# Column halves and quarter tiles in the two recurrent mixers of a four-layer backbone

## The chip, the core and the metric

One core of a Trainium2 chip runs the whole program in one launch. The engines are TensorE (PE in the rows, its weight loads PEld), VectorE (DVE), ScalarE (ACT), GpSimd (POOL) and SyncE (SP, which starts most DMAs). The metric is the device time of one execution in microseconds (us), and the time before is the median of three executions.

## The reference

The program computes four layers on 256 context tokens and 256 latent tokens of width 1024. Each layer is a modulated RMSNorm, a token mixer and a gated residual, then a second norm and a feed-forward part. The mixers are, in order: a bidirectional Mamba-2 scan, a bidirectional RWKV-7 scan, centred pooling, and grouped attention. The change touches the first two. Cut to the lines that matter:

```
# mixer 1, one direction: 32 heads of 64 channels, chunks of 128 tokens
seg   = cum[:, :, :, None] - cum[:, :, None, :]
decay = exp(where(lower, seg, -inf))
cb    = einsum('bcign,bcjgn->bcijg', cm, bm)
w     = cb[..., None] * decay * dt
y     = einsum('bcijge,bcjgep->bcigep', w, x) + (part from the chunks before)
out   = rmsnorm(y * silu(z)) @ out_w            # z = u @ in_w[:, :2048]

# mixer 2, one direction: 16 heads of 64, for every token t
sa = S @ kk_t
S  = S * w_t - outer(sa, kk_t * a_t) + outer(v_t, k_t)
y_t = S @ r_t
```

Mixer 2 is computed in chunks of 64 tokens: products of decayed operands inside a chunk ("grams"), the inverse of a triangular matrix, and a short scan over four chunks.

## The kernel before

The matrix products with weights are made in two parts: `whi` is a weight rounded to fp32r, `wlo` is what is left of it, and each product is three matmuls (L212 to L214). `wsplit` (L200) makes the parts: ScalarE the upper one, and one of the engines in `eng` the lower one (L207).

**Mixer 1** (`mix` and its helpers, L472 to L595). Four groups of eight heads, two steps each. A step takes 256 columns of x (`x_products`), convolves them, and then works on two pairs of heads (`m`). For each head `e` of a pair and each direction `d` it spreads the decays over 128 partitions (L542, L543), takes the exponential on ScalarE (`E`, L548), multiplies it by `cb` on VectorE (`W`, L550), and adds four float32 products into the pair's bank `py` (L553). A head's product has 64 output rows, so it uses one half of TensorE's columns. `gate_z` projects the gate z of a step, with the lower parts of its weights made by the engine in `ZE` (L470), which is GpSimd.

**Mixer 2.** `stage` prepares one direction of a unit (`Unit`: eight heads, of the context, `j` 0, or of the latents, `j` 1). For each chunk, `decays` makes decay products, `operands` the joint operand tile `BK` (two tensors side by side, each head parity with zeros in the rows of the other, L1060 and L1061), `grams` multiplies it (L1077 or L1080) and turns it round (L1089). There are four units with four chunks and two directions each: 32 such steps. `invert` makes the triangular inverse; with `warm` (L1384) it adds 32 products of no use, by `spin` (L1116). `scan` is the recurrence over chunks. Generators of these functions are run in turn by `weave`.

The order on each engine isn't written out by hand: a scheduler places the instructions of all these functions on five queues, each in order, and fills TensorE's queue in mixer 1 with projections of the next step. The pools' buffer counts bound how far it can look ahead.

Of the kernel before, what the change touches and what calls it, by code (L numbers as in the profile page):

```python
# [10 lines left out]
F32 = mybir.dt.float32  # L11
# [4 lines left out]
ALU = mybir.AluOpType  # L16
# [121 lines left out]
def tile_backbone(ctx: ExitStack, tc: tile.TileContext, T, out: bass.AP, dbg=None, stop=99):  # L138
# [227 lines left out]
    with ExitStack() as es:  # L366
# [103 lines left out]
        XE, ZE = (V,), (G,)  # L470
# [25 lines left out]
        def mix(g, s, px, bf, cf, btm, cb):  # L496
# [38 lines left out]
            for m in range(2):  # L535
                mi = 4 * g + 2 * s + m
                py = bank("py", 1)
                for e in range(2):
                    h = hf + 2 * m + e
                    for d in range(2):  # L540
                        pbc = bank("pbc", 2)
                        PE.matmul(pbc, ehb[:, h:h + 1].to_broadcast([96, 128]), parts[d], start=True, stop=False)  # L542
                        PE.matmul(pbc, identb, maskb[:, d:d + 1, :].to_broadcast([128, 4, 128]),  # L543
                                  start=False, stop=True)
                        E = mt.tile([128, NT], F32, name="E")
                        for c in range(4):
                            sl = slice(128 * c, 128 * c + 128)
                            S.activation(E[:, sl], pbc[:, sl], AF.Exp, bias=ncum[:, c, 32 * d + h:32 * d + h + 1])  # L548
                        W = mt.tile([128, NT], F32, name="W")
                        V.tensor_mul(W, E, cb)  # L550
                        for c in range(4):
                            sl = slice(128 * c, 128 * c + 128)
                            PE.matmul(py[64 * e:64 * e + 64, sl], xdt[d][:, c, 128 * m + 64 * e:128 * m + 64 * e + 64],  # L553
                                      W[:, sl], start=d == 0 and c == 0, stop=d == 1 and c == 3,
                                      skip_group_check=True)
                V.tensor_add(yz[:, mi, :], yz[:, mi, :], py)
                for d in range(2):
# [11 lines left out]
                    W = mt.tile([128, NT], F32, name="W")  # L569
# [422 lines left out]
    def stage(tp, rp, F, un, d, l2, nb, bks, tags, ready):  # L992
# [5 lines left out]
        last = 64 if d == 0 else 0  # L998
# [37 lines left out]
        def decays(c):  # L1036
# [7 lines left out]
            S.activation(Dp[:, :, o:o + 64], cum, AF.Exp, scale=-0.3032655)  # L1044
            S.activation(cum, cum, AF.Exp, scale=0.3032655)
            return Dp, cum

        def operands(c, dd, slot):
# [4 lines left out]
            V.tensor_copy(un.dc[d][:, :, c:c + 1], Dp[:, :, last:last + 1])  # L1053
            KR = rp.tile([128, 4, NQ], F32, name=f"KR{slot}")

            BK = bks[d][un.flip[d]]
            un.flip[d] ^= 1
            for par in range(2):
                r, b0 = ROWS[par], 64 * par
                V.scalar_tensor_tensor(BK[par][r, :, b0:b0 + 64], ta[r, :, cl], 0.5, Di[r], op0=ALU.mult, op1=ALU.mult)  # L1060
                G.tensor_mul(BK[par][r, :, 64 - b0:128 - b0], kd[r, :, cl], Di[r])  # L1061
# [4 lines left out]
            return BK  # L1066

        def grams(c, BK, slot):
# [5 lines left out]
            for h in range(4):  # L1074
                for par in range(2):
                    if j:
                        PE.matmul(g[par][:, h, :], BK[par][:, h, :], KR[:, h, :], start=True, stop=True)  # L1077
                    else:
                        for z in range(2):
                            PE.matmul(g[par][ROWS[z], h, :], BK[par][:, h, 64 * z:64 * z + 64], KR[:, h, :],  # L1080
                                      start=True, stop=True)
# [5 lines left out]
            for h in range(4):  # L1087
                for par in range(2):
                    PE.transpose(t[par][:, 64 * h:64 * h + 64], BK[par][ROWS[par], h, :],  # L1089
                                 ident[ROWS[par], ROWS[par]])  # L1090
# [23 lines left out]
    def spin(o, x):  # L1114

        PE.matmul(o[:, :x.shape[1] * x.shape[2]], ident, x, start=True, stop=True)  # L1116

    def invert(tp, un, zbank, slots={}, warm=(0, 0)):

# [69 lines left out]
        for d in range(2):  # L1189
            zb = zbank() if d else z0  # L1190
            z = zb[:, :256].rearrange("p (n t) -> p n t", t=16)
            for n in range(16):
                if warm[0] and n % warm[0] == 0:
                    spin(zb[:, 256:], zp[:, d, n, 0:16].unsqueeze(2).to_broadcast([128, 16, 8]))
                for q in range(4):
                    a, b = (TB[1], zp[:, 1, :, 0:16]) if d else (zp[:, 0], T32[0][:, :, 16:32])
                    PE.matmul(z[QS(q), n, :], a[QS(q), n, :], b[QS(q), n, :], start=True, stop=True)
# [5 lines left out]
        for d in range(2):  # L1203
            cb_ = slice(32 * (1 - d), 32 * (1 - d) + 32)
            z = zbank()
            for n in range(16):
                if warm[1] and n % warm[1] == 0 and n < 13:
                    spin(z[:, 32 * n:], TB[d][:, n, :].unsqueeze(2).to_broadcast([128, 32, 4]))
# [8 lines left out]
        for d in range(2):  # L1217
            cb_ = slice(32 * (1 - d), 32 * (1 - d) + 32)
            z = zbank()
            for n in range(16):  # L1220
                if warm[1] and n % warm[1] == 0 and n < 13:
                    spin(z[:, 32 * n:], T32[d][:, n, :].unsqueeze(2).to_broadcast([128, 32, 4]))
# [85 lines left out]
    def operand_tiles(tp):  # L1308
        t = [[tp.tile([128, 2, 4, 128], F32, name=f"BK{d}{i}") for i in range(2)] for d in range(2)]
        for d in t:  # L1310
            for x in d:
                for par in range(2):
                    G.memset(x[:, par], 0.0)
        return [[[x[:, par] for par in range(2)] for x in d] for d in t]
# [17 lines left out]
    with ExitStack() as es:  # L1332
# [28 lines left out]
        with tc.tile_pool(name="r00", bufs=1, side="right", reuse_waits="tile") as r00, tc.tile_pool(name="tp0", bufs=1, reuse_waits="tile") as tp:  # L1361
# [22 lines left out]
            weave((invert(tp, D0, misc, warm=(2, 4)), 1), *stages(tp, r01, F, D1, 1, bks, (("gr", "xu"), ("acc", "xu")), always))  # L1384
            mark("T01S00")
            slots = {"T": ("BK00", [128, 2, 4, 128]), "M0": ("l2", [128, 2, 512]), "M1": ("BK01", [128, 2, 4, 128])}
# [490 lines left out]
```

## Time and profile before

| | |
|---|---|
| time, median of 3 | 2691.66 us (2684.7 to 2692.46) |
| profiled execution, time | 2704.16 us |
| its span | 2702.3 us, 43164 instructions |
| TensorE, VectorE, ScalarE, GpSimd busy | 92%, 77%, 54%, 15% |
| mean granted TensorE clock | 0.934 |

The stages in the order of time are: mixer 1 (to 478 us), its output projection and the dense feed-forward part (to some 930 us), mixer 2 (to some 1660 us), and then, for nearly all of the remaining 1042 us, the experts, whose weights stream from memory. Within mixer 2 the rows speak of the context's first unit (1005 to 1080), its inverse beside the second unit (1080 to 1165), its scan (1165 to 1240), the latents' first unit (1340 to 1395), and their scan beside the second unit (1440 to 1540). Busy time is that of an engine with at least one instruction in flight. One float32 product of the program stands in the trace as two matmul records (512 for L553, of which the program has 256); a float32 transpose is one.

### The profile page before, as it was taken

The numbers are of one execution on the slowest core, as the hardware profiler recorded it, in microseconds if no ns is written. First come the engines' busy times: TensorE is split into PE (matmuls) and PEld (weight loads), VectorE is DVE, ScalarE is ACT, GpSimd is POOL, SyncE is SP. The second block draws the span as 40 slices with busy tenths as digits, with TensorE's granted clock in tenths as the row PEclk, the third lists the DMA queues.
The fourth block names the chain that finished last, engine by engine and source line by source line (L and its number), as shares of the span: only waits on it lengthen the run. The fifth ranks groups of instructions, "written<-read, shape, count | busy, mean of one in ns | idle before, by whom it ended". The sixth has DMA issues, their size and how long they took to land. (4 is left out here: it accounts for less than half of the span.)

```text
span 2702.3 us, 43164 instructions
## 1 busy us (share of the span) xinstructions
PE 2499.3 (92%) x16810; PEld 2043.9 (76%) x16810; DVE 2070.4 (77%) x3118; ACT 1455.4 (54%) x2290; POOL 416.1 (15%) x506
## 2 busy tenths in 40 slices
PE   7999999999999968768977898999999999999997
PEld 4777776778888867558866687788788788878875
DVE  5777788667454377778696745999899899989997
ACT  4444446333222265336343334878787778778775
POOL 1122132110000156224453221000000000000001
PEclk9999999999999978577887877999999999999998
DMA  7322231335554231012110116699899899989983
GB/s 260 114 86 88 78 102 53 132 110 196 177 196 160 65 110 48 1 42 95 41 63 10 57 34 249 262 360 362 326 372 357 330 362 368 358 320 363 372 340 152
DMA packets 99207, 511.54 MB, mean 189 GB/s; under 512 B 11648, under 2 KB 19072, under 8 KB 55216
## 3 DMA queue, kind: packets, MB, share of 16 engines
q1 hardware_dynamic: 97520, 506.52, 51.1%
q8 instruction: 134, 2.20, 0.3%
q10 hardware_dynamic: 1472, 2.16, 0.3%
q14 instruction: 81, 0.66, 0.1%
HBM read 506.54 MB, written 2.10 MB: 188 GB/s over the span
## 5 line engine op out<-in xcount | busy, mean ns | idle before, releaser
L1734 DVE TENSOR_TENSOR wlo<-wraw,whi 128x1024 fp32r<-128x1024 f32 x662 | 798.4, 1224 | 71.3 <-ACT whi L1733 50.6
L1733 ACT CAST whi<-wraw 128x1024 fp32r<-128x1024 f32 x662 | 694.3, 1051 | 209.2 <-PE gu L214 112.0
L213 PE MATMUL gu<-wlo,xg 128*128 128x512 f32 x896 | 355.7, 397 | 1.5 <-DVE wlo L1734 0.7
L214 PE MATMUL gu<-whi,xg 128*128 128x512 f32 x896 | 350.3, 391 | 0.0
L212 PE MATMUL gu<-whi,xg 128*128 128x512 f32 x896 | 336.8, 392 | 1.1 <-ACT xg L1753 0.9
L206 ACT CAST whi<-wraw 128x1024 fp32r<-128x1024 f32 (+2 forms) x126 | 129.5, 1028 | 229.8 <-PE acc L213 216.4
L207 DVE TENSOR_TENSOR wlo<-wraw,whi 128x1024 fp32r<-128x1024 f32 (+2 forms) x110 | 131.7, 1198 | 106.3 <-ACT whi L206 106.2
L213 PEld LDWEIGHTS gu<-wlo,xg 128*128 128x128 f32 x896 | 168.8, 188 | 42.4 <-DVE wlo L1734 5.8
L212 PEld LDWEIGHTS gu<-whi,xg 128*128 128x128 f32 x896 | 168.7, 188 | 38.2 <-ACT xg L1753 1.6
L214 PEld LDWEIGHTS gu<-whi,xg 128*128 128x128 f32 x896 | 168.9, 188 | 31.6
L213 PE MATMUL y<-wlo,HT 128*128 128x512 f32 x448 | 179.1, 400 | 2.3 <-DVE wlo L1734 2.1
L212 PE MATMUL y<-whi,HT 128*128 128x512 f32 x448 | 177.1, 397 | 3.0 <-DVE xg L1754 3.0
L214 PE MATMUL y<-whi,HT 128*128 128x512 f32 x448 | 176.8, 395 | 0.0
L1808 POOL TENSOR_TENSOR wraw<-yx,SH 128x512 f32<-128x512 f32 x4 | 7.5, 1879 | 1025.4 <-DVE yx L1804 1025.4
L212 PE MATMUL acc<-h2hi,whi 128*128 128x512 f32 x352 | 137.3, 393 | 3.4 <-ACT h2hi L343 3.4
L213 PE MATMUL acc<-h2lo,whi 128*128 128x512 f32 x352 | 137.7, 391 | 0.0
L212 PE MATMUL acc<-hhi,whi 128*128 128x512 f32 (+1 forms) x328 | 135.8, 414 | 0.8 <-ACT whi L206 0.8
L214 PE MATMUL acc<-h2hi,wlo 128*128 128x512 f32 x352 | 135.0, 391 | 0.9 <-DVE wlo L207 0.9
L213 PE MATMUL acc<-hlo,whi 128*128 128x512 f32 (+1 forms) x328 | 134.1, 409 | 0.0
L214 PE MATMUL acc<-hhi,wlo 128*128 128x512 f32 (+1 forms) x328 | 133.8, 409 | 0.0
L305 POOL TENSOR_TENSOR sqa<-sqa,sq 128x512 f32<-128x512 f32 (+1 forms) x35 | 46.8, 1338 | 536.0 <-issue 311.9
L777 POOL TENSOR_TENSOR wlo<-wraw,whi 128x512 fp32r<-128x512 f32 (+1 forms) x69 | 86.1, 1257 | 150.3 <-ACT whi L776 138.9
(575 smaller groups left out, 5550.6 us busy)
## 6 DMA issues: line engine op xcount, KB each, us to landing
wraw<-in_w_mi_dram SPq DMA_DIRECT2D x219, 1024.0 KB, 4.9
wraw<-in_w_mo_dram SPq DMA_DIRECT2D x112, 1024.0 KB, 4.9
wraw<-in_w_modT_dram SPq DMA_DIRECT2D x56, 512.0 KB, 4.1
wraw<-in_w_ffi_dram SPq DMA_DIRECT2D x44, 512.0 KB, 3.6
wraw<-in_w_mod_dram SPq DMA_DIRECT2D x40, 512.0 KB, 4.5
wraw<-in_w_mb_dram SPq DMA_DIRECT2D x40, 512.0 KB, 4.3
wraw<-in_w_mbo_dram SPq DMA_DIRECT2D x16, 512.0 KB, 3.5
wraw<-in_w_ffo_dram SPq DMA_DIRECT2D x16, 512.0 KB, 3.5
```

The costliest lines, as they stand in the source:

```text
L206: S.copy(hi, raw)
L207: eng[q % len(eng)].tensor_sub(lo, raw, hi.bitcast(F32))
L212: PE.matmul(o, whi, xhi, start=start, stop=False)
L213: PE.matmul(o, whi, xlo, start=False, stop=False)
L214: PE.matmul(o, wlo, xhi, start=False, stop=stop)
L305: G.tensor_add(self.acc, self.acc, sq)
L777: self.eng[self.n % len(self.eng)].tensor_sub(lo, raw, hi.bitcast(F32))
L1733: S.copy(hi, raw[:, k:k + 2, :])
L1734: V.tensor_sub(lo, raw[:, k:k + 2, :], hi.bitcast(F32))
L1808: G.tensor_mul(xf[:, tt, 512 * n:512 * n + 512], fs, fg[:, 512 * n:512 * n + 512])
```

## The change

Four edits:

- In mixer 1 both heads of a pair are prepared for one direction, and then their products are issued in turn, one head, the other head, for each chunk of 128 tokens. `W` has four buffers instead of two.
- The lower parts of the gate's weights are made by VectorE (`ZE`).
- In mixer 2 `BK` holds two tensors of 64 columns without zeros: one VectorE and one GpSimd instruction over 128 partitions make it. Grams and turning are products of 64 rows by 64 columns, a quarter of the array. The end value of the decays (`dc`), a VectorE copy before, is an exponential on ScalarE. The memsets of the zeros (L1313) go.
- `spin` and its calls go from `invert`.

```
-        XE, ZE = (V,), (G,)
+        XE, ZE = (V,), (V,)
...
-                for e in range(2):
-                    h = hf + 2 * m + e
-                    for d in range(2):
+                for d in range(2):
+
+                    Ws = []
+                    for e in range(2):
+                        h = hf + 2 * m + e
...
-                        W = mt.tile([128, NT], F32, name="W")
+                        W = mt.tile([128, NT], F32, name="W", bufs=4)
                         V.tensor_mul(W, E, cb)
-                        for c in range(4):
-                            sl = slice(128 * c, 128 * c + 128)
+                        Ws.append(W)
+                    for c in range(4):
+                        sl = slice(128 * c, 128 * c + 128)
+                        for e in range(2):
                             PE.matmul(py[64 * e:64 * e + 64, sl], xdt[d][:, c, 128 * m + 64 * e:128 * m + 64 * e + 64],
-                                      W[:, sl], start=d == 0 and c == 0, stop=d == 1 and c == 3,
+                                      Ws[e][:, sl], start=d == 0 and c == 0, stop=d == 1 and c == 3,
...
+            end = 63 * o
+            S.activation(un.dc[d][:, :, c:c + 1], cum[:, :, end:end + 1], AF.Exp, scale=-0.3032655)
...
-            V.tensor_copy(un.dc[d][:, :, c:c + 1], Dp[:, :, last:last + 1])
...
-            for par in range(2):
-                r, b0 = ROWS[par], 64 * par
-                V.scalar_tensor_tensor(BK[par][r, :, b0:b0 + 64], ta[r, :, cl], 0.5, Di[r], op0=ALU.mult, op1=ALU.mult)
-                G.tensor_mul(BK[par][r, :, 64 - b0:128 - b0], kd[r, :, cl], Di[r])
+            V.scalar_tensor_tensor(BK[:, :, 0], ta[:, :, cl], 0.5, Di, op0=ALU.mult, op1=ALU.mult)
+            G.tensor_mul(BK[:, :, 1], kd[:, :, cl], Di)
...
+        def side(BK, par, h, z):
+
+            return BK[ROWS[par], h, z ^ par, :]
...
-                    if j:
-                        PE.matmul(g[par][:, h, :], BK[par][:, h, :], KR[:, h, :], start=True, stop=True)
-                    else:
-                        for z in range(2):
-                            PE.matmul(g[par][ROWS[z], h, :], BK[par][:, h, 64 * z:64 * z + 64], KR[:, h, :],
-                                      start=True, stop=True)
+                    for z in range(2):
+                        PE.matmul(g[par][ROWS[z], h, :], side(BK, par, h, z), KR[ROWS[par], h, :], start=True, stop=True)
...
-                    PE.transpose(t[par][:, 64 * h:64 * h + 64], BK[par][ROWS[par], h, :],
-                                 ident[ROWS[par], ROWS[par]])
+                    for z in range(2):
+                        PE.matmul(t[par][ROWS[z], 64 * h:64 * h + 64], side(BK, par, h, z),
+                                  ident[ROWS[par], ROWS[par]], start=True, stop=True)
...
-            weave((invert(tp, D0, misc, warm=(2, 4)), 1), *stages(tp, r01, F, D1, 1, bks, (("gr", "xu"), ("acc", "xu")), always))
+            weave((invert(tp, D0, misc), 1), *stages(tp, r01, F, D1, 1, bks, (("gr", "xu"), ("acc", "xu")), always))
...
-        t = [[tp.tile([128, 2, 4, 128], F32, name=f"BK{d}{i}") for i in range(2)] for d in range(2)]
-        for d in t:
-            for x in d:
-                for par in range(2):
-                    G.memset(x[:, par], 0.0)
-        return [[[x[:, par] for par in range(2)] for x in d] for d in t]
+        return [[tp.tile([128, 4, 2, 64], F32, name=f"BK{d}{i}") for i in range(2)] for d in range(2)]
```

TensorE's queue in mixer 1, second step of the first group, before (numbers are buffers: `W_1194` and `W_1208` belong to one head, for the two directions; the other head's products stand 24 rows further on):

```order
L508 MATMUL misc_1138<-cst_75,xs_1124 128x128 x4
L553 MATMUL py_1185<-W_1194,xdt0_1101 64x128 x4
L553 MATMUL py_1185<-W_1208,xdt1_1102 64x128 x4
L560 LDWEIGHTS ehw_318
L560 MATMUL pbc_1254<-parts1_389,ehw_318 128x512
L212 MATMUL acc_1458<-hhi_314,whi_1449 128x512
```

The same place in the changed kernel (L553 is L557 there; `W_1194` and `W_1204` are the two heads):

```order
L508 MATMUL misc_1138<-cst_75,xs_1124 128x128 x4
L557 MATMUL py_1185<-W_1194,xdt0_1101 64x128
L557 MATMUL py_1185<-W_1204,xdt0_1101 64x128
L557 MATMUL py_1185<-W_1194,xdt0_1101 64x128
L557 MATMUL py_1185<-W_1204,xdt0_1101 64x128
```

Products that stood four to a head now stand in turn. Over all of mixer 1 the changed queue has the 256 products in 62 runs: six of 8, twenty-one of 7, three of 6, two of 5, one of 3, four of 2 and twenty-five of 1.

TensorE's queue in the context's first inverse, before (L1116 is `spin`):

```order
L1116 MATMUL ms<-T,cst 128x128
L1197 MATMUL ms<-T,M_9366 32x16 x8
L1116 MATMUL ms<-M_9367,cst 128x128
L1211 MATMUL ms<-M_9367,C_8239 32x32
L1211 MATMUL ms<-M_9367,C_8240 32x32
```

And in the changed kernel (L1197 and L1211 are L1192 and L1204; L1013 and L1014 are the low-rank products of the second unit, L1010 and L1011 before):

```order
L1192 MATMUL ms<-T,M_9414 32x16 x11
L1013 MATMUL xu<-hw_7502,l_9098 128x128
L1014 MATMUL xu<-ha_7504,l_9098 128x128
L1192 MATMUL ms<-T,M_9414 32x16 x13
L1013 MATMUL xu<-hw_7503,l_9098 128x128
L1014 MATMUL xu<-ha_7505,l_9098 128x128
L1192 MATMUL ms<-T,M_9414 32x16 x38
L1204 MATMUL ms<-M_9415,C_8231 32x32
```

The useless products are gone, and low-rank products that stood ahead of the inverse before stand among its own.

VectorE's queue in the latents' first unit, before:

```order
L1053 COPY dc0_12234<-Dp0_12332 128x4
L1064 TENSOR_TENSOR KR2_12409<-r_10359,Dp0_12332 128x4x64
L1060 SCALAR_TENSOR_TENSOR BK01_12223<-ta0_12243,cum0_12330 64x4x64 x2
L1084 TENSOR_TENSOR C0_12236<-gr_12358,c2_7463 128x512
L1084 TENSOR_TENSOR C1_12237<-gr_12359,c2_7463 128x512
```

And after (L1060 is L1061, L1064 is L1065, L1084 is L1085):

```order
L1065 TENSOR_TENSOR KR2_12486<-r_10415,Dp0_12379 128x4x64
L1061 SCALAR_TENSOR_TENSOR BK01_12279<-ta0_12291,cum0_12377 128x4x64
L1085 TENSOR_TENSOR C0_12284<-gr_12404,c2_7463 128x512
L1085 TENSOR_TENSOR C1_12285<-gr_12405,c2_7463 128x512
L1063 TENSOR_TENSOR KR2_12486<-kk_10414,Dp0_12379 128x4x64
```

The copy and one of the two operand instructions are gone, and the rest keeps its order.

## Rows read from the trace of the kernel before

**Rows 1.** Windows by stage: length, busy time (instructions), granted clock, DMA.
```profile
core 0: us, PE busy (x) PEld busy (x) DVE busy (x) ACT busy (x) POOL busy (x), PEclk, DMA share, GB/s
62.00:478.00 416.00, 404.30 (x2252) 303.61 (x2251) 328.86 (x578) 196.82 (x462) 99.91 (x78) 1.00 0.25 87
1005.00:1080.00 75.00, 65.88 (x632) 56.73 (x630) 52.24 (x100) 43.58 (x117) 47.32 (x74) 0.89 0.18 62
1080.00:1115.00 35.00, 17.20 (x188) 14.65 (x188) 34.67 (x102) 15.46 (x48) 10.16 (x16) 0.70 0.00 1
1115.00:1153.00 38.00, 37.60 (x576) 28.86 (x576) 15.84 (x30) 7.59 (x16) 8.07 (x13) 0.50 0.01 2
1340.00:1395.00 55.00, 41.52 (x401) 35.91 (x401) 45.47 (x82) 24.39 (x70) 35.62 (x50) 0.90 0.08 30
1440.00:1540.00 100.00, 84.26 (x1217) 73.82 (x1211) 68.08 (x163) 41.89 (x115) 28.47 (x46) 0.84 0.07 25
```

**Rows 2.** Timeline of TensorE, mixer 1: start, length (us), instructions merged.
```profile
150.95 1.96 PE L553 MATMUL py<-W,xdt 128*64 128x128 f32 x16
120.48 1.04 PE L243 MATMUL acc<-wraw,cc 128*2 128x256 f32 x14
```

**Rows 3.** Groups of lines, TensorE in 62 to 480 us: count, busy, mean ns, idle before.
```profile
L553 PE MATMUL py<-W,xdt 128*64 128x128 f32 x512 | 67.7, 278 | 1.3 <-DVE xdt L511 1.3
```

**Rows 4.** Timeline of TensorE, mixer 2: products and transposes at the full clock.
```profile
1166.48 0.64 PE L1242 MATMUL xu<-Sz,KR 128*64 128x64 f32 x16
1162.38 0.47 PE L1089 MATMUL xu<-cst,BK 64*128 64x64 f32 x8
1348.52 1.95 PE L1077 MATMUL gr<-KR,BK 128*128 128x128 f32 x16
```

**Rows 5.** Line 243: ns least/median/most, first and last start.
```profile
L243 PE MATMUL acc<-wraw,cc x320: 377/379/634, 12.8 to 362.6; 128*2 128x256 f32 x160
```

**Rows 6.** Line 1242, its first form.
```profile
L1242 PE MATMUL xu<-Sz,KR x512: 219/222/368, 1165.5 to 1622.6; 128*64 128x64 f32 x171
```

**Rows 7.** Groups of lines, 62 to 480 us: lower weight parts by engine.
```profile
L207 DVE TENSOR_TENSOR wlo<-wraw,whi 128x1024 fp32r<-128x1024 f32 x24 | 30.0, 1251 | 8.5 <-ACT whi L206 8.5
L207 POOL TENSOR_TENSOR wlo<-wraw,whi 128x1024 fp32r<-128x1024 f32 x16 | 41.6, 2603 | 90.3 <-ACT whi L206 90.3
```

**Rows 8.** Timeline of VectorE and GpSimd around 392 us.
```profile
391.58 3.53 DVE L461 SCALAR_TENSOR_TENSOR cy<-cv,cwh,cy 128x512 f32<-128x512 f32 x2
391.98 2.58 POOL L207 TENSOR_TENSOR wlo<-wraw,whi 128x1024 fp32r<-128x1024 f32 x1 [3.20 <-ACT whi L206]
```

**Rows 9.** Line 461, as in rows 5.
```profile
L461 DVE SCALAR_TENSOR_TENSOR cy<-cv,cwh,cy x96: 653/748/2944, 59.4 to 401.5; 128x512 f32<-128x512 f32 x96
```

**Rows 10.** Timeline of TensorE in the context's first inverse.
```profile
1119.33 0.41 PE L1197 MATMUL ms<-M,T 32*32 32x16 f32 x16
1119.67 0.80 PE L1116 MATMUL ms<-T,cst 128*128 128x128 f32 x2
1142.24 0.64 PE L1211 MATMUL ms<-M,C 32*32 32x32 f32 x16
1142.81 0.80 PE L1116 MATMUL ms<-M,cst 128*128 128x128 f32 x2
1143.54 0.64 PE L1225 MATMUL ms<-M,T 32*32 32x32 f32 x16
```

**Rows 11.** Timeline of VectorE in the same inverse, with its waits.
```profile
1138.38 0.70 DVE L1215 TENSOR_SCALAR T<-ms 32x512 f32<-32x512 f32 x1 [4.55 <-ACT T L1214]
```

**Rows 12.** Groups of lines, the whole program: operands of mixer 2.
```profile
L1061 POOL TENSOR_TENSOR BK<-kd,cum 64x256 f32<-64x256 f32 x64 | 55.2, 863 | 53.1 <-PE xu L1089 20.1 <-ACT cum L1045 17.9 <-DVE kd L1021 7.5
L1060 DVE SCALAR_TENSOR_TENSOR BK<-ta,cum 64x256 f32<-64x256 f32 x64 | 38.9, 608 | 6.2 <-PE xu L1089 4.7 <-ACT cum L1045 0.6
L1053 DVE COPY dc<-Dp 128x4 f32<-128x4 f32 x32 | 14.1, 440 | 1.4 <-ACT Dp L1044 1.2
L1045 ACT ACTIVATE cum<-cum 128x256 f32<-128x256 f32 x32 | 13.0, 414 | 1.0
```

More of the change, by code (lines that the diff above doesn't have):

```diff
@@ L568, in mix @@
                         PE.matmul(p[:, sl], st[d][c][:, 128 * m:128 * m + 128], cf[:, sl], start=True, stop=True)
-                    W = mt.tile([128, NT], F32, name="W")
+                    W = mt.tile([128, NT], F32, name="W", bufs=4)
                     for sl in ((slice(128, 512),) if d == 0 else (slice(0, 128), slice(256, 512))):
@@ L997, in stage @@
         o = 1 - d
-        last = 64 if d == 0 else 0
         gr, ms = (lambda: bank(tags[0], 2)), (lambda: bank(tags[1], 2))
@@ L1112, in stage, with invert @@
             yield from grams(c, BK, 2 * i + d)
-    def spin(o, x):
-        PE.matmul(o[:, :x.shape[1] * x.shape[2]], ident, x, start=True, stop=True)
-    def invert(tp, un, zbank, slots={}, warm=(0, 0)):
+    def invert(tp, un, zbank, slots={}):
         def tile_(name, n):
@@ L1192, in invert @@
             for n in range(16):
-                if warm[0] and n % warm[0] == 0:
-                    spin(zb[:, 256:], zp[:, d, n, 0:16].unsqueeze(2).to_broadcast([128, 16, 8]))
                 for q in range(4):
@@ L1206, in invert @@
             for n in range(16):
-                if warm[1] and n % warm[1] == 0 and n < 13:
-                    spin(z[:, 32 * n:], TB[d][:, n, :].unsqueeze(2).to_broadcast([128, 32, 4]))
                 for par in range(2):
@@ L1220, in invert @@
             for n in range(16):
-                if warm[1] and n % warm[1] == 0 and n < 13:
-                    spin(z[:, 32 * n:], T32[d][:, n, :].unsqueeze(2).to_broadcast([128, 32, 4]))
                 for par in range(2):
@@ L1383, in tile_backbone @@
             mark("A01T00")
-            weave((invert(tp, D0, misc, warm=(2, 4)), 1), *stages(tp, r01, F, D1, 1, bks, (("gr", "xu"), ("acc", "xu")), always))
+            weave((invert(tp, D0, misc), 1), *stages(tp, r01, F, D1, 1, bks, (("gr", "xu"), ("acc", "xu")), always))
             mark("T01S00")
-            slots = {"T": ("BK00", [128, 2, 4, 128]), "M0": ("l2", [128, 2, 512]), "M1": ("BK01", [128, 2, 4, 128])}
+            slots = {"T": ("BK00", [128, 1024]), "M0": ("l2", [128, 2, 512]), "M1": ("BK01", [128, 1024])}
             gi = invert(tp, D1, misc, slots)
```

## The prediction

> **What bounds the kernel now.** I read the windows by stage first, then the groups of lines inside a stage, then single stretches of the timeline for the rate of one kind of instruction. The chain that ended last covers only the end of the program, so it says nothing here. In mixer 1 TensorE is busy 404.3 of 416 us and VectorE 328.9, so TensorE idles 12 us there, VectorE 87 [rows 1]: what leaves TensorE leaves the stage, until VectorE is the next to bind. Mixer 2 has a different limit in each stage. From 1080 to 1115 VectorE is busy 34.7 of 35 us; from 1115 to 1153 TensorE is, 37.6 of 38, at a granted clock of 0.50 throughout, that is 1.2 GHz; from 1340 to 1395 and from 1440 to 1540 neither is full over the whole stage, and both wait for each other in turn [rows 1]. The experts and the feed-forward parts are not touched, so I take their 1500 us as they are.
>
> **Term 1, heads in turn in mixer 1.** Sixteen passes of L553 take 1.96 us, the last of them some 0.28 [rows 2, 3]: (1.96 - 0.28)/15 = 0.112 us each, one after the other, all on one column half while a head's run lasts. Whether passes on different halves run at once can be read elsewhere. L1242 alternates halves with 64 columns to stream: (0.64 - 0.22)/15 = 0.028 us a pass [rows 4, 6], where 64 columns alone should take half of 0.112, 0.056. So two run together. L243 uses four column groups and streams 256 columns: (1.04 - 0.38)/13 = 0.051 us a pass [rows 2, 5], against 0.224 alone, so there four run together. In the changed queue a run of n products takes as long as its odd or even half, 2 x (n/2 rounded up) passes: 6 x 8 + 21 x 8 + 3 x 6 + 2 x 6 + 4 + 4 x 2 + 25 x 2 = 308 slots instead of the 512 passes [rows 3], so 204 x 0.112 = 22.8 us less on TensorE. The ends: 0, if other waits fill it, and 22.8. Each pair now needs two E and two W before its first product. TensorE's queue has projections to go on with, but behind a pair that waits they wait too. I take 16 us.
>
> **Term 2, lower parts on VectorE.** Sixteen instructions move. On VectorE they cost 16 x 1.25 = 20.0 us, on GpSimd they took 41.6 [rows 7]. They weren't free for VectorE there: beside the GpSimd instruction at 391.98, two L461 took 3.53 us together, where the median of one is 0.75 [rows 8, 9]; the second ended only after GpSimd did. That is 2.0 us lost under one of the sixteen, if all are like it 32. So the move costs VectorE between 20 - 16 x 2.0 = -12 us and +20 us. I take 0 on the path: the stage has 87 us of VectorE to spare, and the value that came from GpSimd after 2.6 us now comes after 1.25. If that cover goes, it is the first rival.
>
> **Term 3, useless products out of the inverse.** Each of the 32 holds TensorE for 0.73 us (1142.81 to 1143.54), between groups of sixteen useful passes of 0.34 or 0.57 us [rows 10]: 32 x 0.73 = 23.4 us of the 38 from 1115 to 1153. TensorE is the one waited for: VectorE and ScalarE each idle some 4.5 us before each part of the chain [rows 11]. What is late next is VectorE, which has 15.8 us of work in the stretch [rows 1], mostly at its start: about 7 us of it (after term 4) stands ahead of the inverse's second step, then come 16 groups of 0.57 us, 9 us, and about 2 us of evictions: 18 to 20 instead of 38. The low-rank products that the queue now has among them are work that was done before 1115 and is not added. The ends are 10 us (VectorE sets the pace) and 23. I take 18. They kept no clock up: it was at its lower level for all of their 38 us.
>
> **Term 4, operands of mixer 2.** VectorE loses 64 - 32 instructions of 0.61 us and 32 copies of 0.44 [rows 12]: 19.5 + 14.1 = 33.6 us, or 1.05 for each of the 32 steps. Both are long for their size, as GpSimd's L1061 runs beside them, like the pair in [rows 8]; that halves too, 55.2 to some 28 us [rows 12], and 24 memsets go. ScalarE gains 32 small exponentials, at most 0.41 each, the time of one 64 times as wide (L1045) [rows 12], 13 us in all, and it is under 60% busy in each of these stages [rows 1]. But they stand ahead of the factor that the operands wait for: up to 0.41 a step, 3 us a stage, which I leave in the range.
>
> TensorE pays and gains. A step turns its operand with eight passes now, (0.47 - 0.22)/7 = 0.036 us each, 0.29 us [rows 4], its last taken as long as that of L1242, and with 32 then. Its grams are 32 passes of 0.028 us, 0.9, in the context's half, and 16 of 0.112, 1.8, in the latents' [rows 4]; then 32 quarter passes in both. No row shows four quarters. L243 shows four column groups at once, L1089 two row halves at once (a pass of 64 columns each 0.036). If quarters run four at a time, a pass of 64 columns costs 0.014 and one of 128 columns 0.028: turning 0.45, grams 0.45 and 0.9, so the steps change by 0.9 - 0.9 - 0.29 = -0.29 and 1.35 - 2.09 = -0.74 us, 16 times each, -16 us. If only two run at once, turning is 0.9 and the grams stay, +0.61 each, +20 us. I take the first, since both directions of splitting are seen to run side by side.
>
> The Trainium skill (TensorEngine Tiling (Array Packing), Overview and Key Properties) says that a 64 by 64 split gives four tiles which load and multiply independently; by it TensorE's change would be the -16 us. The same page (Restrictions and Gotchas) says that a column split excludes transpose mode for float32, which would be why turning takes plain products of two passes here; by that rule the price of turning would stand whatever the overlap. No run here shows either.
>
> By stage: 1005 to 1080, 8.4 us less on VectorE and 2 on TensorE, of which TensorE's own work hides half: 4. From 1080 to 1115, VectorE is the bound and holds four steps: 4 x 1.05 = 4 us; I count 2, as the last steps after 1153 give some back. From 1340 to 1395, VectorE loses 7 to 8 us, full from 1355 on: 5. From 1440 to 1540 both lose 6 to 8, between the scan's waits: 4. That is 15.
>
> **Term 5, the clock.** With fewer passes per step TensorE is less busy in mixer 2, where the granted clock already is 0.50 to 0.90 [rows 1]. A scan's products at 1.2 GHz take longer; I count 2 us lost, between 0 and 6.
>
> **Sum.** 16 + 0 + 18 + 15 - 2 = 47 us. The profiled execution took 2704.2 us for a span of 2702.3, 12.5 us (0.5%) over the median of the runs shown; 2704.2 - 47 = 2657.2 for it, and 2691.7 - 47 = 2644.7 for the median. I predict 2645.
>
> **Rivals.**
> 1. VectorE takes mixer 1 over. For: 328.9 us of work plus 20, in order, against a TensorE reduced to 381; TensorE's queue is in order as well. Against: 32 us still lie between them. Then nothing but the last runs of term 1 arrives: 2645 + 16 = 2661.
> 2. Quarters run two at a time. For: no row shows four. Term 4 then costs TensorE 36 us more than counted; in the first and last stage, where it is 84 to 88% busy, and at the inverse's end about 40% of it lies on the path, 14 us: 2659.
> 3. All of it arrives. Term 1 in full (+7), term 4 at VectorE's full 8 us in each of its three stages (+10): 2628.
> 4. Slower: quarter products leave TensorE so little at work that the clock falls to 1.2 GHz through the stages at 1005, 1340 and 1440, 230 us with 192 of TensorE [rows 1]. For: the inverse's stretch, which TensorE filled with passes on small tiles and useless products, had 0.50 throughout, so being busy isn't enough. Against: the stage at 1440, with a scan's half-array products among the grams, has 0.84. Passes then take twice as long; with half of the 192 us stretched by 0.84/0.50 = 1.7 on the path, 65 us are lost: 2710. It decides from 47 us on, about 70% of those stages at the lower level.
> 5. Heads in turn don't overlap with 128 columns, because the pairs are broken up: 2661, as the first.
>
> **How the numbers follow.** Forecast 0.52, rivals 0.12, 0.14, 0.12, 0.06 and 0.04. Less than 0.3% (8 us) can't be told from no change. Faster by more: the forecast, rivals 1, 2, 3 and 5, less what combinations of them leave over, 0.87; within: 0.07, rivals 1 and 2 together with a clock that costs its 6 us; slower: 0.06. The range goes from 2622 (rival 3 and a little) to 2676 (rivals 1 and 2 together, 2645 + 16 + 14).
>
> **What would show it.** Right: pairs of products in L557 that start together and sixteen of them in about 1 us; mixer 1 ending near 462 instead of 478 us; about 20 us from the inverse's first product to its last eviction; VectorE's time on operands near half of 38.9 us and no copy of `dc`; sixteen passes of grams in about 0.45 us. Wrong: TensorE idle over 30 us in mixer 1 with VectorE full; quarter passes 0.028 us apart with 64 columns; a granted clock of 0.5 in the stages at 1340 and 1440.

## The result, and the profile after

The changed kernel took 2655.2 us (median of 4 runs, 2652.9 to 2655.6) beside 2689.6 of the kernel before: ratio 0.987, 95% interval 0.9855 to 0.989, so 34 us less (30 to 39). 2645 was forecast. The profiled execution took 2652.9 us for a span of 2651.0.

The first profile of before (2704.2 us) lay 12 to 15 us above its own median. So the stages below are compared with a second profile of before, of 2685.6 us, taken later (the run x3_before). The first fence is that one, the second the changed kernel; columns as in [rows 1]. The rows are mixer 1, the context's first unit, the stretch up to the first inverse's first product, that inverse (two rows of after), the latents' first unit, and their second unit beside the scan.

```profile
62.00:479.00 417.00, 405.67 (x2253) 305.09 (x2251) 328.96 (x578) 196.87 (x462) 100.45 (x78) 0.99 0.25 86
1006.00:1076.00 70.00, 64.19 (x614) 56.02 (x613) 50.55 (x99) 40.31 (x108) 47.31 (x74) 0.85 0.19 63
1076.00:1114.00 38.00, 20.43 (x201) 17.30 (x199) 36.82 (x103) 18.34 (x57) 10.17 (x16) 0.70 0.00 1
1114.00:1162.00 48.00, 46.43 (x742) 36.60 (x744) 21.29 (x43) 13.83 (x31) 14.00 (x30) 0.56 0.01 2
1318.00:1381.00 63.00, 49.99 (x608) 42.73 (x607) 53.41 (x100) 25.08 (x78) 40.69 (x60) 0.95 0.08 27
1435.00:1515.00 80.00, 69.21 (x1067) 60.35 (x1066) 55.09 (x109) 37.36 (x103) 28.58 (x46) 0.93 0.01 2
```

```profile
62.00:457.00 395.00, 380.94 (x2252) 280.62 (x2250) 323.45 (x594) 195.72 (x461) 59.89 (x62) 0.99 0.28 91
985.00:1056.00 71.00, 62.93 (x822) 54.78 (x820) 49.31 (x114) 45.23 (x128) 37.61 (x56) 0.86 0.19 63
1056.00:1079.00 23.00, 6.24 (x160) 5.32 (x159) 23.00 (x61) 7.42 (x25) 6.73 (x11) 0.59 0.00 1
1079.00:1107.00 28.00, 23.26 (x588) 20.45 (x588) 14.96 (x27) 16.43 (x43) 6.56 (x10) 0.50 0.01 4
1107.00:1118.00 11.00, 8.49 (x291) 8.06 (x288) 5.27 (x13) 6.97 (x17) 4.85 (x14) 0.66 0.01 4
1281.00:1346.00 65.00, 49.18 (x936) 40.56 (x932) 45.38 (x82) 23.89 (x80) 33.98 (x52) 0.84 0.01 2
1404.00:1484.00 80.00, 70.75 (x1358) 60.43 (x1359) 49.73 (x93) 38.52 (x112) 22.57 (x38) 0.87 0.01 3
```

The reader is to see three things. Mixer 1 is 22 us shorter and TensorE, still its bound, gave all of it (405.7 to 380.9 busy). The first inverse fell from 48 to 39 us, not to 30. The latents' two units took as long as before (63 and 65, 80 and 80), though VectorE worked 8 and 5 us less in them.

Between matching events, the stretches of the two profiles in us (start and end read from the timelines; "forecast" is the prediction's own term). The inverse begins with a chain of short VectorE steps; its matrix products follow. "Features" are the products that prepare the inputs of the latents' units. The latents' first unit starts within the stretch listed before it, so these two overlap.

| stretch | before, second profile | after | change | forecast |
|---|---|---|---|---|
| start to end of mixer 1 | 479.5 | 457.6 | -21.9 | -16 |
| context's first unit, low-rank to inverse's start | 48.6 | 37.9 | -10.7 | -4 |
| from there to the end of VectorE's chain | 58.5 | 55.1 | -3.4 | -2 |
| first inverse's products, to the scan's first | 48.0 | 38.9 | -9.1 | -18 |
| scan beside the latents' features | 135.2 | 146.5 | +11.3 | clock: +2 for all |
| from there to the latents' first gram | 43.3 | 40.6 | -2.7 | |
| latents' first unit, low-rank to last masked gram | 62.8 | 65.3 | +2.5 | -5 |
| latents' second unit | 80.3 | 79.7 | -0.6 | -4 |
| whole span | 2683.7 | 2651.0 | -32.7 | -47 |

Mixer 1 in rows of after: a run of products of two heads in turn, the group of all 512 (before in [rows 3]), and VectorE's lower parts ([rows 7]).

```profile
208.58 1.31 PE L557 MATMUL py<-W,xdt 128*64 128x128 f32 x20
L557 PE MATMUL py<-W,xdt 128*64 128x128 f32 x512 | 44.6, 281 | 1.0 <-DVE W L552 0.9
L207 DVE TENSOR_TENSOR wlo<-wraw,whi 128x1024 fp32r<-128x1024 f32 x40 | 49.4, 1235 | 11.4 <-ACT whi L206 11.2
```

Twenty passes in 1.31 us are (1.31 - 0.28)/19 = 0.054 us each, half of the 0.112 before: two run at once. The group's busy time fell by 67.7 - 44.6 = 23.1 us, where 22.8 was worked out.

Mixer 2 in rows of after: quarter products of 64 and of 128 columns at the full clock, and the groups that answer to [rows 12].

```profile
1031.07 0.63 PE L1082 MATMUL acc<-KR,BK 64*64 64x64 f32 x30
1304.78 1.10 PE L1082 MATMUL gr<-KR,BK 64*64 64x128 f32 x32
L1062 POOL TENSOR_TENSOR BK<-kd,cum 128x256 f32<-128x256 f32 x32 | 29.6, 927 | 40.4 <-ACT cum L1050 21.3 <-PE xu L1091 7.8 <-DVE kd L1024 5.7
L1061 DVE SCALAR_TENSOR_TENSOR BK<-ta,cum 128x256 f32<-128x256 f32 x32 | 17.6, 554 | 1.0 <-PE gr L1082 0.6
L1049 ACT ACTIVATE dc<-cum 128x4 f32<-128x4 f32 x32 | 6.2, 195 | 3.2 <-DVE cum L1043 3.2
```

A pass of 64 columns takes (0.63 - 0.22)/29 = 0.014 us, one of 128 (1.10 - 0.28)/31 = 0.026: four quarters at once. The Trainium skill (TensorEngine Tiling (Array Packing), Overview and Key Properties) says that a 64 by 64 split gives four tiles that work independently; these rows agree. VectorE's operand time went from 38.9 to 17.6 us, GpSimd's from 55.2 to 29.6, and the copy of `dc` (14.1) became 6.2 on ScalarE.

### The profile page after: what moved, and what is told of

Read it like the earlier page. It is cut to its first block, busy times and chain, and to the rows that moved or that the text cites. A ratio compares the mean times of both kernels' runs of the same rounds, so it can differ in the third digit from the quotient of the medians.

```text
span 2651.0 us, 44915 instructions
## 1 busy us (share of the span) xinstructions
PE 2439.0 (92%) x17770; PEld 1992.1 (75%) x17770; DVE 2039.2 (77%) x3070; ACT 1458.8 (55%) x2322; POOL 342.4 (13%) x434
## 5 line engine op out<-in xcount | busy, mean ns | idle before, releaser
L207 DVE TENSOR_TENSOR wlo<-wraw,whi 128x1024 fp32r<-128x1024 f32 (+2 forms) x126 | 151.1, 1200 | 109.3 <-ACT whi L206 109.1
L781 POOL TENSOR_TENSOR wlo<-wraw,whi 128x512 fp32r<-128x512 f32 (+1 forms) x69 | 87.7, 1281 | 156.1 <-ACT whi L780 108.7
```

What stands on the lines that cost most here:

```text
L207: eng[q % len(eng)].tensor_sub(lo, raw, hi.bitcast(F32))
L781: self.eng[self.n % len(self.eng)].tensor_sub(lo, raw, hi.bitcast(F32))
```

## Experiments

All kernels timed, in us against the kernel before of the same series (ratio's difference from 1 times that median), with 95% intervals:

| kernel | what it has of the change | median | change |
|---|---|---|---|
| s1_heads | heads in turn | 2690.4 | -5.4 (-8.4 to -2.2) |
| s2_gate | gate on VectorE | 2696.5 | +3.2 (-0.5 to +7.0) |
| s3_nospin | no useless products | 2679.7 | -17.8 (-24.3 to -11.3) |
| s4_quarter | joint operands, quarter tiles | 2690.8 | -2.7 (-6.2 to +0.8) |
| p1_mixer1 | heads, gate | 2661.3 | -31.8 (-37.2 to -26.7) |
| p2_mixer2 | no useless products, quarter tiles | 2668.6 | -21.8 (-26.4 to -17.0) |
| p3_spinback | all but the removal of the useless products | 2669.8 | -22.1 (-26.7 to -17.5) |
| p4_all | the changed kernel again | 2655.5 | -36.9 (-42.8 to -31.2) |
| x1_bank | all, and other banks for one direction | 2642.0 | -51.1 (-56.2 to -46.0) |
| x2_noquarter | all but quarter tiles | 2663.0 | -26.4 (-30.9 to -21.8) |
| y1_nogate | all but the gate | 2659.0 | -35.6 (-41.2 to -29.9) |

**Single edits.** Each is its part of the change alone. s1_heads:

```
-                for e in range(2):
-                    h = hf + 2 * m + e
-                    for d in range(2):
+                for d in range(2):
...
+                    for c in range(4):
+                        sl = slice(128 * c, 128 * c + 128)
+                        for e in range(2):
```

> Only mixer 1's heads in turn (and four W buffers) on the kernel before. Theory A (the prediction's terms, as the profile after corrects them): mixer 1 is worth what its end moved, 21 us, and by itself: 2689.6 - 21 = 2669. Theory B: the gate's lower parts on VectorE have a share in the 21 us (they took GpSimd's weight off VectorE), and the heads alone bring the 16 us that I took or less: 2674 to 2680, and the gate alone then shows a gain of 5 or more.

s2_gate:

```
-        XE, ZE = (V,), (G,)
+        XE, ZE = (V,), (V,)
```

> Only the lower parts of the gate's weights on VectorE. Theory A: 0, 2686 to 2693, as TensorE bounds mixer 1 and VectorE has 87 us to spare. Theory B: values that come 1.3 us earlier and a VectorE that isn't held by GpSimd bring 5 us or more, 2685 or less. Theory C: 20 us more on VectorE, in order, lose 3 us or more: over 2693.

s3_nospin:

```
-            weave((invert(tp, D0, misc, warm=(2, 4)), 1), *stages(tp, r01, F, D1, 1, bks, (("gr", "xu"), ("acc", "xu")), always))
+            weave((invert(tp, D0, misc), 1), *stages(tp, r01, F, D1, 1, bks, (("gr", "xu"), ("acc", "xu")), always))
```

> Only the 32 useless products out of the first inverse. Theory A (the prediction): -18, 2672, if TensorE sets the pace there. Theory B (read from the profile after, where the same stretch got 9 us shorter): -9 or less, 2680 or more, since VectorE's work and the low-rank products of the next unit fill the stretch, the more so in this kernel as its operands on VectorE are still the long ones.

s4_quarter has the change's lines in `decays`, `operands`, `grams` and `operand_tiles`:

```
-        t = [[tp.tile([128, 2, 4, 128], F32, name=f"BK{d}{i}") for i in range(2)] for d in range(2)]
+        return [[tp.tile([128, 4, 2, 64], F32, name=f"BK{d}{i}") for i in range(2)] for d in range(2)]
```

> Only the joint operands and quarter tiles of mixer 2 (with the end values on ScalarE); the useless products stay. Theory A (the prediction): -15, 2675, of which 9 in the latents' two stages. Theory B (read from the profile after): -15 or more, all of it between 1005 and 1115 us where VectorE is the bound, nothing in the latents' stages. Theory C: the useless products and the operands depend on each other, either alone brings less than its share, and the four single edits add up to clearly less than the 34 us of all four together.

The useless products were worth the forecast's 18. The heads and the quarter tiles missed, and the gate can't be told from the forecast's 0. The sum of the four is -22.7, against -34 and -37 for all together. In s1_heads mixer 1 does end at 460.3 us, 19 earlier than in the second profile of before, but the stretch up to the end of VectorE's chain took 66.3 us instead of 58.5, and the stages behind it lost most of the rest. That stretch in the second profile of before, then in s1_heads:

```profile
1055.18:1113.71 58.53, 38.20 (x461) 32.92 (x459) 51.81 (x137) 30.94 (x91) 22.13 (x36) 0.78 0.00 1
1036.73:1103.06 66.33, 46.31 (x489) 40.66 (x487) 57.16 (x146) 34.24 (x97) 25.04 (x39) 0.68 0.01 1
```

The code of these stages is the same, their order isn't: VectorE, the busiest engine there, has 146 instructions in it instead of 137, 57.2 us of work instead of 51.8, and the granted clock is lower. The scheduler places the whole program anew for every edit.

**Pairs, the useless products put back, and the whole.** p1_mixer1 joins the first two edits, p2_mixer2 the others, p4_all is the changed kernel, p3_spinback has `warm=(2, 4)` back in it.

> Both edits of mixer 1 (heads in turn, gate's lower parts on VectorE), nothing of mixer 2. Alone they measured -5 and +3 us by their ratios. Theory A, they simply add: -2, 2690 to 2694 beside 2695 of before. Theory B, they need each other (with TensorE less full, GpSimd's slow lower parts are what it waits for; in the profile of all four edits mixer 1 ends 2.6 us earlier than with the heads alone): -8 or more. Theory C: mixer 1 does end 18 to 21 us earlier, but the granted clock of the stages behind it takes most of it back; then the profile shows mixer 1's end near 458 and stages of mixer 2 that lose 10 us or more against before at a lower granted clock.

> Both edits of mixer 2 (joint operands in quarter tiles, no useless products), nothing of mixer 1. Alone they measured -3 and -18 us. Theory A, they add: -21. Theory B, they help each other: without the useless products the inverse's stretch took 29 us in the profile but the stage after it grew, as VectorE's long operands are next there; with the short ones -26 or more. Theory C, they overlap, since both shorten the same stretch where VectorE and TensorE wait in turn: -18 or less.

> The changed kernel with the 32 useless products put back into the first inverse (heads in turn, gate on VectorE, joint operands stay). Theory A (removing them is worth 18 whatever else is done): 34 - 18 = 16 us faster than before. Theory B (they are worth more when the operands are short): 8 or less faster than before. Theory C (worth 9, as the inverse's stretch of the changed kernel was 9 us shorter in the profile): 25 faster.

> The changed kernel as it is, timed beside the others, for the sum and for a second profile. Theory A, the four single edits add up (-5 + 3 - 18 - 3 = -23): 2668 to 2676, and the 34 of the first timing was high. Theory B, they help each other: -31 to -38, 2657 to 2664. The second profile also tells how much the stages vary from one execution to the next: if the stage times of mixer 2 differ by more than 5 us from the first profile's, single profiles don't settle the latents' stages.

p1_mixer1 gained 31.8, although its mixer 1 ends at 457.2, only 3 us before that of s1_heads. So some 23 of the 26 us between the two don't lie in mixer 1. Only a part can be located: the profile of s1_heads is the fastest of its eleven executions and that of p1_mixer1 the slowest of its four, 14 us apart, with 3 to 5 us each in the stretch above, in the scan beside the features and in the latents' first stage. The pair of mixer 2 simply adds. The useless products cost 36.9 - 22.1 = 15 in company, though without them the inverse is 21 us shorter (59.5 and 38.9); the scan and the features behind it, read below, take some 8 of that back. The intervals of p4_all and of the first timing agree. Together: 31.8 + 21.8 = 53.6 for the pairs, 37 for both, so some 17 us of such a comparison belong to no edit.

Two things behind this can be read. The first is one stretch of untouched code, the scan beside the latents' features. Its length has two groups: 132 to 139 us in eight profiles (before 138.8 and 135.2, s1_heads, s3_nospin, p1_mixer1 134.8, p2_mixer2, p3_spinback, x1_bank 137.2), and 145 to 147 in six (s2_gate, s4_quarter, x2_noquarter, y1_nogate, and the changed kernel both times, 146.5 and 146.3). But the queue doesn't put the same work into it each time: 1474 matmul records in the second profile of before, 1592 in the changed kernel. With the stretch behind it, up to the latents' first gram, the records agree (2170 to 2172 with the old operands, 2186 to 2223 with quarter tiles), so this sum can be compared. It lies between 178 and 188 us, and the higher the granted clock, the shorter it is: 178 to 179 us at 0.86 and 0.87 (x3_before, p1_mixer1, p3_spinback), 181 to 186 at 0.82 to 0.84 (the first profile of before, s1_heads, s3_nospin, p2_mixer2, x1_bank, y1_nogate), 186 to 188 at 0.79 to 0.81 (the other five). First fence: both stretches, and pieces of 10 us inside them, in the second profile of before; second: the same in the changed kernel.

```profile
1161.73:1340.18 178.45, 147.24 (x2171) 130.24 (x2171) 137.64 (x307) 78.79 (x191) 66.01 (x86) 0.86 0.21 67
1262.00:1272.00 10.00, 9.73 (x128) 8.36 (x127) 9.10 (x19) 7.05 (x15) 2.77 (x4) 0.50 0.16 56
1272.00:1282.00 10.00, 8.02 (x32) 6.62 (x30) 9.80 (x21) 5.89 (x15) 2.96 (x2) 0.50 0.33 107
1282.00:1292.00 10.00, 10.00 (x62) 7.81 (x62) 9.93 (x17) 6.04 (x14) 5.29 (x5) 1.00 0.23 74
```

```profile
1117.67:1304.78 187.11, 159.83 (x2221) 140.75 (x2219) 140.15 (x304) 77.92 (x192) 62.78 (x79) 0.79 0.20 64
1218.00:1228.00 10.00, 10.00 (x181) 8.30 (x182) 8.48 (x17) 6.62 (x14) 3.73 (x4) 0.50 0.17 57
1228.00:1238.00 10.00, 8.64 (x33) 6.63 (x33) 9.28 (x20) 5.04 (x13) 3.85 (x2) 0.67 0.31 92
1238.00:1248.00 10.00, 10.00 (x31) 7.07 (x31) 6.19 (x12) 2.66 (x6) 2.53 (x2) 0.50 0.09 27
1248.00:1258.00 10.00, 10.00 (x157) 9.15 (x156) 7.75 (x16) 4.85 (x11) 1.27 (x1) 0.50 0.27 93
```

Both fall to 0.50, that is 1.2 GHz, with TensorE busy 8.0 to 10 of every 10 us. In this profile of before it is back at 2.4 GHz after 20 us, in the changed kernel it stays low for most of 40. The changed kernel did this twice (187.1 and 186.9 us for the sum), but the kernel before had 185.7 at 0.82 and 178.5 at 0.86 with one and the same queue, so order alone doesn't decide it. What does was not found, and no run changed the clock by itself: that the clock makes the length is argued from these rows, not shown.

The second thing is the first inverse. By kernel, from the end of VectorE's chain to the scan's first product: 48 us with the useless products and old operands (before, s1_heads, p1_mixer1), 29 to 30 without the products (s3_nospin, x2_noquarter), 60 with the products and quarter tiles (s4_quarter, p3_spinback), 38 to 39 without the products and with quarter tiles (p2_mixer2, the changed kernel, y1_nogate). So quarter tiles cost 8 to 12 us there, about as much as they gain before it. The timeline of TensorE in the changed kernel says how (start, length, instructions merged; the last row is the inverse's last product):

```profile
1079.36 0.72 PE L1192 MATMUL ms<-M,T 32*32 32x16 f32 x36 [4.19 <-DVE T L1182]
1080.00 0.80 PE L1013 MATMUL xu<-hw,l 128*128 128x128 f32 x2
1080.59 0.63 PE L1014 MATMUL xu<-ha,l 128*128 128x128 f32 x2
1081.15 0.29 PE L1192 MATMUL ms<-M,T 32*32 32x16 f32 x4
1081.38 0.80 PE L1013 MATMUL xu<-hw,l 128*128 128x128 f32 x2
1081.96 0.63 PE L1014 MATMUL xu<-ha,l 128*128 128x128 f32 x2
1082.53 0.60 PE L1192 MATMUL ms<-M,T 32*32 32x16 f32 x26
1105.24 1.92 PE L1216 MATMUL ms<-M,T 32*32 32x32 f32 x64 [0.17 <-DVE T L1208]
```

Between the inverse's products (L1192) stand eight such pairs of low-rank products (L1013, L1014) of the second unit's later half, 1081.15 - 1080.00 = 1.15 us each at 1.2 GHz: 9.2 us in the chain that everything waits for. p3_spinback, with the useless products, has them there too. In s3_nospin, x2_noquarter and the kernel before they stand ahead of it. What holds them back in the changed kernel's order is a buffer: both directions' low-rank products and turnings share the two buffers of `xu`.

**Low-rank products ahead of the inverse, and quarter tiles taken out.** x1_bank changes one word:

```
-            weave((invert(tp, D0, misc), 1), *stages(tp, r01, F, D1, 1, bks, (("gr", "xu"), ("acc", "xu")), always))
+            weave((invert(tp, D0, misc), 1), *stages(tp, r01, F, D1, 1, bks, (("gr", "xu"), ("acc", "ms")), always))
```

> The changed kernel with one word more: the second direction of the context's second unit takes its buffers for low-rank products and turning from the banks of the first inverse (ms), instead of sharing xu with the first direction. By the order of the queue its 16 low-rank products of the second half then stand ahead of the inverse's first product, as in the kernel without useless products alone, and no longer between the inverse's products. Theory A (those products in the queue, at the lower clock, are what made the inverse's stretch 39 us instead of 29): first product to last eviction falls from 25.7 to about 18 us, the scan starts 8 to 10 us earlier, 2645 to 2648. Theory B (work only moves: VectorE's steps or a tighter ms bank take its place): the scan starts within 3 us of where it did, 2652 to 2659. Theory C: the stretch gets shorter and the granted clock of the scan's stage behind it takes 5 us or more of it back.

x2_noquarter is the changed kernel with the operands, grams and turning of before (the hunk of s4_quarter left out).

> Mixer 1's two edits and no useless products, but the operands of mixer 2 as before (zeros, full-height grams, end values copied by VectorE). Theory A (joint operands are worth 3 or 4 us, as they were alone and beside the other edit of mixer 2): 2658 to 2661. Theory B (worth nothing or less: what they gain before the inverse they lose in it): 2645 to 2655. Theory C (worth the 15 of the prediction once TensorE and VectorE are less loaded): 2668 to 2672.

x3_before is the kernel before, once more.

> The kernel before once more, unchanged, for a second profile. Theory A: the first profile (2704.2) was a slow draw, and what it has over the median of 2692 lies in the experts (783.5 and 255.2 us in their two stretches, where the other kernels of this series had 777 to 778 and 253 to 254 for the same code) and in the stages of mixer 2 at a lower granted clock; the second then has 8 to 12 us less in these and the same ends of mixer 1 (478 +- 2) and of the first inverse's stretch (48 +- 1). Theory B: the stages of mixer 1 vary as well, by 5 us or more, and single profiles tell nothing of them.

TensorE's timeline of x1_bank in the same inverse:

```profile
1082.42 1.26 PE L1192 MATMUL ms<-M,T 32*32 32x16 f32 x128
1083.55 0.50 PE L1192 MATMUL ms<-T,M 32*32 32x16 f32 x39
1085.96 1.38 PE L1192 MATMUL ms<-T,M 32*32 32x16 f32 x89 [1.91 <-issue]
1090.47 1.92 PE L1204 MATMUL ms<-M,C 32*32 32x32 f32 x64 [3.14 <-DVE M L1195]
1093.31 1.92 PE L1204 MATMUL ms<-M,C 32*32 32x32 f32 x64
1095.09 3.45 PE L1216 MATMUL ms<-M,T 32*32 32x32 f32 x128
```

No low-rank product stands among these; the last four pairs stand in the 5 us before them. The stretch takes 29.3 us instead of 38.9, the 9.6 of theory A, and from the first product to the last 16.1 us (1082.42 to 1098.54) instead of 27.8 (1079.36 to 1107.16). That is more than the 9.2 of the pairs, and the granted clock is 0.69 there, where the changed kernel has 0.54. But the short stretch doesn't need that clock: s3_nospin and x2_noquarter, which have no low-rank products there either, take 29.0 and 30.2 us at 0.53 and 0.51.

The kernel takes 2642.0 us, 51 less than before (46 to 56), where the changed kernel has 37 (31 to 43). Where the other 5 us or so lie can't be read, as its profile (2649.5) is the slowest of its five executions and only 3.3 us shorter than that of the changed kernel: it gains the 9.6 and 3 in the scan and the features with the stretch behind them (183.9 at 0.82 against 187.1 at 0.79), and loses 5 in the experts (783.2 against 777.8), which no edit touches, and some more in the latents' stages.

x2_noquarter lies between theories A and C: quarter tiles are worth 36.9 - 26.4 = 10.5 in company (8 with the first timing), 4 beside the removal alone, 2.7 by themselves (an interval with 0 in it), and -10 beside the edits of mixer 1 where the useless products stay (p1_mixer1 against p3_spinback). Removing the useless products from p1_mixer1, which gives x2_noquarter, shows no gain (31.8 and 26.4, with intervals that overlap), though it shortens the inverse from 47.9 to 30.2 us: the scan and the features with the stretch behind them went from 178.1 us at 0.87 to 187.1 at 0.79, on the same 2170 and 2172 records, and the stretch of the latents' scan and second unit from 145.3 to 150.6.

x3_before took 2685.6 us: theory A. Mixer 1 ends at 479.5 and the inverse takes 48.0 as in the first profile; the 18.6 us between the two are 6 in the experts and 12 in mixer 2's later stages.

**The gate back on GpSimd.**

```
-        XE, ZE = (V,), (V,)
+        XE, ZE = (V,), (G,)
```

> The changed kernel with the lower parts of the gate's weights back on GpSimd; the other three edits stay. Alone the move to VectorE measured +3 us, beside the heads it made 2690 into 2661. Theory A (mixer 1's end: with the heads in turn TensorE waits for GpSimd's slow lower parts; the profile gave 2.9 us of it): mixer 1 ends 3 us later than 457.5, and the total is 3 us more than the changed kernel, 2656 to 2661. Theory B (the 26 us between heads alone and heads with the gate belong to the gate's work itself): 2675 or more, with mixer 1's end or mixer 2's first stage late by 10 us or more. Theory C (those 26 us are a matter of the queue's order and the granted clock in the stages behind, which each edit draws anew): mixer 1 ends within 4 us of 457.5, and the total lies anywhere from -5 to +15 of the changed kernel with the difference in stages of mixer 2 whose granted clock differs.

Its mixer 1, columns as before:

```profile
62.00:462.00 400.00, 384.43 (x2250) 279.33 (x2249) 332.49 (x577) 196.39 (x461) 99.13 (x78) 0.99 0.27 90
```

Mixer 1 ends at 462.2, so the gate's edit is worth 4.6 us there (3 between s1_heads and p1_mixer1), and VectorE is busy 332.5 us where it is 323.5 with 16 instructions of 1.235 us more: if the difference is theirs, each of GpSimd's sixteen had cost the others (332.5 - 323.5 + 19.8)/16 = 1.8 us. The total is 0 to 4 us from that of the changed kernel. Theory A fits nearly (4.6 us instead of 3, and a total inside its 2656 to 2661); of theory C the total fits, and mixer 1's end is 0.7 us outside its 4; B, that the 26 us between s1_heads and p1_mixer1 are the gate's, falls.

## Why the prediction was right, and where it was not

- **Term 1 (-16).** Right in its mechanism and nearly in size. Pairs run at once (0.054 us a pass), the group gave 23.1 where 22.8 was worked out, and mixer 1 ended 17 to 19 us earlier by the heads (y1_nogate and s1_heads against the second profile of before). The list of runs in the section on the change adds up to 259 products instead of 256; by the order in the trace the same sum gives 300 slots and 23.7 us, so nothing rests on the slip. TensorE idles 14 us of 395 in mixer 1, so rivals 1 and 5 are out.
- **Term 2 (0).** 3 to 5 us in mixer 1 beside the heads, nothing alone, and in the total nothing that can be told from 0. The loss under GpSimd, 2.0 us taken from [rows 8, 9], comes out at 1.8.
- **Term 3 (-18).** Right alone (-17.8; inverse 48 to 29 us), and in company the removal shortens the inverse by 21 us as well (59.5 in p3_spinback, 38.9 in the changed kernel). But the changed kernel's inverse is only 9 us shorter than before's, as the new order that comes with the quarter tiles lengthens it by some 10, and here a step failed: "The low-rank products that the queue now has among them are work that was done before 1115 and is not added." They are added, as they stand in TensorE's queue between products that wait for each other: 8 x 1.15 = 9.2 us. x1_bank took them out and got 9.6 back.
- **Term 4 (-15).** The rates were right (0.014 and 0.026 us a pass, VectorE's share halved; rival 2 is out), the places were not. The context's first unit gave 10.7 instead of 4 and the stretch behind it 3.4, but the 9 of the latents' two units came to nothing. There VectorE is not full, and what it lost in work it gained in waits. Rows of the waits in the latents' first unit (engine, what it waits for, total, times, longest), first of the second profile of before, then of the changed kernel:

```profile
POOL kd L1018 <- ACT ta L1014: 5.0, 3, 2.6
DVE C L1084 <- PE gr L1077: 1.3, 1, 1.3
DVE C L1084 <- PE acc L1077: 0.3, 1, 0.3
```

```profile
POOL kd L1021 <- ACT ta L1017: 17.0, 6, 5.5
DVE C L1085 <- PE acc L1082: 5.3, 2, 4.3
DVE C L1085 <- PE gr L1082: 2.4, 1, 2.4
```

  VectorE waited 1.6 us for grams there and waits 7.7 now, GpSimd 17.0 us for ScalarE instead of 5.0, with a granted clock of 0.84 instead of 0.95. Which of these sets the length isn't shown. That nothing was gained doesn't hang on one profile: from the latents' first gram to the second unit's later low-rank products the seven profiles with quarter tiles took 145 to 152 us and the seven without 145 to 151, at 0.78 to 0.85 and 0.82 to 0.87, though VectorE's work is some 98 instead of 108 us.
- **Term 5 (+2, 0 to 6).** Too small and sought in the wrong place. Rival 4 did not come: the stages at 985, 1281 and 1404 have 0.84 to 0.87. But the scan beside the features, which no edit touches, took 8.7 us longer together with the stretch behind it, at 0.79 instead of 0.86.
- **The sum.** Forecast 47, 33 in the profile against the second one of before, 34 and 37 in the two timings. By the table the inverse gave 8.9 too little, the latents 10.9, and the scan with the features and the stretch behind them cost 6.7 more than the 2 counted for the clock; mixer 1 gave 5.9 more than forecast, term 4's first two stretches 8.1: 12 to 13 net of the 14 between 47 and 33. Errors on both sides made the total nearer than its terms, and that is luck. Rival 3, all of it, did not arrive; the 2642.0 of x1_bank shows where a part of it was.

## What to carry to other kernels

Where a scheduler places the queue anew, read in the new order what stands between the products of a dependent chain: work that has only moved there costs its full time, and one buffer name can move it out again. Don't add up single edits: each draws a new order for the rest of the program, which here was worth some 23 us between two of the kernels, more than most of the edits; judge a term by the length of its own stretch, with the granted clock beside it. And take a second profile of the kernel before, since the first may be 12 us off its own median.

## What the runs showed of the hardware

TensorE was busy 8.6 to 10 of every 10 us at a granted clock of 0.50 for most of 40 us, in a stretch that one profile of the kernel before passed with 20 us at 0.50; over fourteen profiles of untouched code the length went with the granted clock, from 178 us at 0.87 to 188 at 0.79. Two column halves run side by side with 128 columns (0.054 against 0.112 us a pass), and four quarters with 64 and 128 columns (0.014 and 0.026). Two profiles of the same kernel differed by 18.6 us, none of it in mixer 1 or the first inverse.
